# Row sums of a 64 MiB array: one load in place of four for the first row, and a store split into 104 and 24 partitions

## The chip, the cores and the metric

The kernel runs on one core of one Trainium2 chip. The metric is the device time of one execution in microseconds (us); less is better. A core has five engines with instruction queues of their own: TensorE, VectorE (DVE in the profile), ScalarE (ACT), GpSimd (POOL) and SyncE (SP). Data moves between HBM and the on-chip memory (128 partitions) by 16 DMA engines. A DMA is issued by an instruction of an engine's queue; here SyncE issues all loads and the last store, ScalarE the other store.

## The reference

The input is 32 x 512 x 1024 numbers in float32 (67.11 MB), and each run of 1024 is summed:

```python
def reference(x: np.ndarray) -> np.ndarray:
    return np.sum(x, axis=-1).astype(np.float32)
```

There are 16,384 sums of 1024 numbers, 128 for each of the 128 partitions. Nearly all of the work is to read the input once.

## The kernel before, in words

The 16,384 rows are cut into two blocks (`BLOCKS`): the first with 112 rows for each partition, the second with 16. Within a block, partition p holds consecutive rows, so one partition's share of a load is one run of memory. `out_b` and `res` are a block's output in HBM and its tile of sums.

The first block is streamed in seven tiles of `G` = 16 rows for each partition (64 KB for each partition, 8 MiB together), through three buffers of the tile `xt`. The loads are issued by SyncE in the order of the code. The first three tiles find their buffers free; each later load waits until VectorE has summed the tile that was in its buffer (`rows_dve`, one `tensor_reduce` at line 43 for each tile). In the seventh tile ScalarE sums the last 7 rows (`rows_act`, line 51, one instruction with an accumulator for each row), and VectorE the first 9.

The first tile is loaded in two steps (lines 79 to 85). The first of its 16 rows comes by four loads: each takes every fourth partition, 32 in all, 4 KB from each. The fifth load brings the other 15 rows, 60 KB for each of the 128 partitions. All the other tiles of the first block come by a single load of 128 partitions.

After the seventh tile, ScalarE issues the store of the first block's sums (line 91): 128 partitions with 112 sums, 448 bytes, each. It follows ScalarE's own seven rows in ScalarE's queue, waits for VectorE's nine, and has other rows of ScalarE behind it. At that time the loads of the second block are still under way, so the store runs beside them, inside the stream.

The second block's 16 rows come by five loads that get smaller (9, 4 and 2 rows, then the last row in two parts at `CUT` = 544), so that little work is left when the last byte lands. VectorE and ScalarE share them. The last row is summed by VectorE with `pairs_dve` (line 59), and SyncE issues the last store (line 116).

The instructions are scheduled by a planner as written, with one change by hand: after compiling, the first `EARLY` loads of SyncE are taken from the body of the program and put into the entry block, ahead of SyncE's part of the barrier at the start:

```python
loads = [i for i in code if i.engine == sp][:EARLY]
for load in loads:
    assert load.opcode == "DMACopy" and not load.sync_info.on_wait
    code.remove(load)
...
code[at:at] = loads
```

`EARLY` is 5 before: the four loads of the first row and the load of the other 15. SyncE issues the loads of the second and third tile after the barrier.

Of the kernel before, what the change touches and what calls it, by code (L numbers as in the profile page):

```python
# [1 line left out]

# [4 lines left out]

F32 = mybir.dt.float32
ADD = mybir.AluOpType.add
COPY = mybir.ActivationFunctionType.Copy  # L10
X = mybir.AxisListType.X

BLOCKS = (112, 16)
G = 16
ACT_ROWS = 7
CUT = 544
EARLY = 5


@with_exitstack  # L20
def row_sums(
    ctx: ExitStack,
    tc: tile.TileContext,
    x: bass.AP,
    out: bass.AP,
):
    nc = tc.nc
    P = nc.NUM_PARTITIONS

    x_flat = x.flatten_outer_dims()  # L30
    R, D = x_flat.shape
    C = R // P
    assert R % P == 0 and sum(BLOCKS) == C
    out_flat = out.rearrange("a (b c) -> (a b c)", c=1)

    xpool = ctx.enter_context(tc.tile_pool(name="x", bufs=3))
    rpool = ctx.enter_context(tc.tile_pool(name="res", bufs=1))
    part = rpool.tile([P, 1], F32, name="part")
    seen = rpool.tile([P, 1], F32, name="seen")
    pairs = [rpool.tile([P, D // 2], F32, name=f"pairs{i}") for i in range(3)]  # L40

    def rows_dve(xt, res, j, n, c):
        nc.vector.tensor_reduce(  # L43
            out=res[:, c : c + n],
            in_=xt[:, j * D : (j + n) * D].rearrange("p (j d) -> p j d", d=D),
            axis=X,
            op=ADD,
        )

    def sum_act(v, acc):  # L50
        nc.scalar.activation(out=v, in_=v, func=COPY, accum_out=acc)  # L51

    def rows_act(xt, res, j, n, c):
        for i in range(n):
            sum_act(xt[:, (j + i) * D : (j + i + 1) * D], res[:, c + i : c + i + 1])

    def pairs_dve(xt, a, b, first, acc, pairs):
        h = (a + b) // 2
        nc.vector.tensor_tensor_reduce(  # L59
            out=pairs[:, 0 : h - a], in0=xt[:, a:h], in1=xt[:, h:b], scale=1.0, scalar=first,  # L60
            op0=ADD, op1=ADD, accum_out=acc,
        )

    def block(r0, n):
        x_b = x_flat[r0 : r0 + P * n].rearrange("(p c) d -> p (c d)", p=P)
        out_b = out_flat[r0 : r0 + P * n].rearrange("(p c) -> p c", p=P)
        return x_b, out_b, rpool.tile([P, n], F32, name=f"res{r0}")

    full = C - G
    done = 0  # L70
    for b, n in enumerate(BLOCKS):
        x_b, out_b, res = block(done * P, n)
        final = b == len(BLOCKS) - 1
        whole = n - G if final else n
        c = 0
        while c < whole:
            m = min(G, whole - c)
            xt = xpool.tile([P, G * D], F32, tag="xt", name="xt")
            parts = [(slice(None), 0, m)]
            if done + c == 0:  # L80
                parts = [(slice(q, P, 4), 0, 1) for q in range(4)] + [(slice(None), 1, m)]
            for q, i, k in parts:
                nc.sync.dma_start(
                    out=xt[q, i * D : k * D], in_=x_b[q, (c + i) * D : (c + k) * D]
                )
            a = ACT_ROWS if done + c + m == full else 0
            rows_dve(xt, res, 0, m - a, c)
            rows_act(xt, res, m - a, a, c + m - a)
            c += m
        if not final:  # L90
            nc.scalar.dma_start(out=out_b, in_=res)
        done += n

    xt = xpool.tile([P, G * D], F32, tag="xt", name="xt")
    cuts = [0, 9, 13, 15]
    for i, k in zip(cuts, cuts[1:]):
        nc.sync.dma_start(out=xt[:, i * D : k * D], in_=x_b[:, (c + i) * D : (c + k) * D])  # L97
    last = 15 * D
    for i, k in ((0, CUT), (CUT, D)):
        nc.sync.dma_start(  # L100
            out=xt[:, last + i : last + k],
            in_=x_b[:, c * D + last + i : c * D + last + k],
        )

    for i, k in zip(cuts[:2], cuts[1:3]):
        h = (k - i) // 2
        rows_dve(xt, res, i, h, c + i)
        rows_act(xt, res, i + h, k - i - h, c + i + h)
    pairs_dve(xt, 13 * D, 14 * D, 0.0, res[:, c + 13 : c + 14], pairs[2])
    rows_act(xt, res, 14, 1, c + 14)  # L110
    pairs_dve(xt, last, last + CUT, 0.0, part, pairs[0])


    nc.vector.tensor_copy(out=seen, in_=part)  # L114
    pairs_dve(xt, last + CUT, last + D, part, res[:, c + 15 : c + 16], pairs[1])
    nc.sync.dma_start(out=out_b, in_=res)


def kernel(tc: tile.TileContext, x: bass.AP, out: bass.AP):
    row_sums(tc, x, out)  # L120
    tc.close()
    tc.compile()  # L122

    sp = mybir.EngineType.SP
    fn = tc.nc.m.functions[0]
    entry, body = None, None
    for blk in fn.blocks:
        ops = [i for i in blk.instructions if i.engine == sp]  # L130
        if entry is None:
            entry = blk
        elif any(i.opcode == "DMACopy" for i in ops):
            body = blk
            break
    code = list(body.instructions)
# [4 lines that stand above are left out]
    body.instructions = code  # L141
    code = list(entry.instructions)
    at = next(k for k, i in enumerate(code) if i.engine == sp and i.opcode == "Drain")
    code[at:at] = loads
    entry.instructions = code

# [1 line left out]
_INS = ['x']  # L148
_OUTS = [((32, 512), 'float32')]


# [23 lines left out]
```

## Time and profile before

| What | us |
|---|---|
| Median of three runs | 163.91 (163.80 to 163.95) |
| The profiled execution's own time | 163.95 |
| Its span (first to last instruction) | 162.2 |
| VectorE busy | 121.5, 16 instructions |
| ScalarE busy | 17.2, 31 instructions |
| One `tensor_reduce` of a whole tile (line 43) | 17.22 |
| First of them starts | 23.59 into the span |
| Store of the first block issued (line 91) | 149.44, lands 7.6 later |
| Last store issued (line 116) | 159.82, lands 1.4 later |

The profile is taken in one execution, whose time is a little longer than its span, by what lies before the first and after the last instruction. Busy times of engines leave out the instructions that issue DMAs and that wait. The DMA share is the mean busy share of the 16 DMA engines; a packet is one partition's run of bytes in a load or store, or the 4 bytes with which a DMA engine reports that its part of a DMA is done. 2208 packets moved 67.18 MB in all. The queue q1 is that of SyncE's DMAs and q10 that of ScalarE's.

### The profile page before, as it was taken

The page shows a single profiled execution, that of the slowest core. Times are in us where ns is not written, and L with a number is a line of the kernel's source. Part 1 is how long each engine was busy: PE and PEld are TensorE (multiplying, and loading weights), DVE is VectorE, ACT ScalarE, POOL GpSimd, SP SyncE. Part 2 cuts the span into 40 slices and gives each one's busy share as a digit, 9 for nine tenths or more (in the row PEclk, how much of TensorE's full clock was granted, in tenths as well). Part 3 has the DMA queues.
Part 4 walks back from the last instruction along what each step waited for, and adds up shares of the span by engine and source line. Part 5 has one row for each costly group of instructions (what it writes and reads, how often), then busy time and mean ns, then how long its engine had stood idle before and what let it go on. Part 6 is the DMA issues. An engine that isn't in the chain of part 4 may idle for free.

```text
span 162.2 us, 126 instructions
## 1 busy us (share of the span) xinstructions
DVE 121.5 (75%) x16; ACT 17.2 (11%) x31; POOL 0.2 (0%) x4
## 2 busy tenths in 40 slices
DVE  0000019999599986999589994999949999598883
ACT  0000000000000000000000000000000000596892
POOL 0000000000000000000000000000000000000000
DMA  7999799889989979969969959969979979998991
GB/s 220 394 485 455 318 456 517 388 388 517 420 356 517 469 307 517 501 275 517 501 275 517 517 259 517 517 275 501 517 307 469 517 323 453 437 418 366 427 393 45
DMA packets 2208, 67.18 MB, mean 414 GB/s; under 512 B 544, under 2 KB 672, under 8 KB 928
## 3 DMA queue, kind: packets, MB, share of 16 engines
q1 hardware_dynamic: 2064, 67.12, 96.5%
q10 hardware_dynamic: 144, 0.06, 0.1%
HBM read 67.11 MB, written 0.07 MB: 414 GB/s over the span
## 4 chain that ended last, share of the span: by engine, by line
DMA 73%; DVE 22%; SPq 0%; issue 0%; DVEq 0%
DMA xt<-in_x_dram 73%; DVE res L43 21%; DVE pairs L59 1%; SPq L97 0%; DVE seen L114 0%; DVE part L59 0%; DVEq L122 0%; DVE res L59 0%
## 5 line engine op out<-in xcount | busy, mean ns | idle before, releaser
L43 DVE TENSOR_REDUCE res<-xt 128x16 f32<-128x16384 f32 (+3 forms) x9 | 119.8, 13309 | 38.0 <-DMA xt<-in_x_dram 38.0
L51 ACT ACT_TABLE_LOAD x1 | 1.3, 1283 | 139.8 <-DMA xt<-in_x_dram 139.8
L51 ACT ACTIVATE xt<-xt 128x1024 f32<-128x1024 f32 x15 | 15.6, 1043 | 2.2 <-DMA xt<-in_x_dram 2.1
L51 ACT ACTIVATION_READ_ACCUMULATOR xt<-xt 128x1 f32 x15 | 2.8, 187 | 0.0
L59 DVE CUSTOM_DVE_ANT_0 pairs<-xt 128x512 f32<-128x512 f32 (+1 forms) x2 | 1.1, 568 | 0.2 <-DMA xt<-in_x_dram 0.2
L59 DVE CUSTOM_DVE_ANT_0 pairs<-xt,part 128x240 f32<-128x240 f32 x1 | 0.5, 469 | 0.0
L114 DVE COPY seen<-part 128x1 f32<-128x1 f32 x1 | 0.2, 153 | 0.0
L59 DVE DVE_READ_ACCUMULATOR2_ANT res<- 128x1 f32 x2 | 0.2, 84 | 0.0
L159 POOL MEMSET const-bfloat16-1.0<- 128x1 bf16 x1 | 0.1, 102 | 0.0
L159 POOL MEMSET const-uint8-127<- 128x1 uint8 x1 | 0.1, 102 | 0.0
L159 POOL MEMSET const-float32-0.0<- 128x1 f32 x1 | 0.1, 99 | 0.2 <-issue 0.2
L159 POOL MEMSET const-float32-1.0<- 128x1 f32 x1 | 0.1, 99 | 0.0
L59 DVE DVE_READ_ACCUMULATOR2_ANT part<- 128x1 f32 x1 | 0.1, 84 | 0.0
## 6 DMA issues: line engine op xcount, KB each, us to landing
xt<-in_x_dram SPq DMA_DIRECT2D x1, 7680.0 KB, 21.0
xt<-in_x_dram SPq DMA_DIRECT2D x1, 4608.0 KB, 32.4
xt<-in_x_dram SPq DMA_DIRECT2D x1, 2048.0 KB, 36.9
xt<-in_x_dram SPq DMA_DIRECT2D x1, 1024.0 KB, 39.0
xt<-in_x_dram SPq DMA_DIRECT2D x4, 128.0 KB, 2.5
xt<-in_x_dram SPq DMA_DIRECT2D x1, 272.0 KB, 39.2
xt<-in_x_dram SPq DMA_DIRECT2D x1, 240.0 KB, 39.3
xt<-in_x_dram SPq DMA_DIRECT2D x6, 40.8
```

The costliest lines, as they stand in the source:

```text
L43: nc.vector.tensor_reduce(out=res[:, c : c + n], in_=xt[:, j * D : (j + n) * D].rearrange("p (j d) -> p j d", d=D), axis=X, op=ADD,)
L51: nc.scalar.activation(out=v, in_=v, func=COPY, accum_out=acc)
L59: nc.vector.tensor_tensor_reduce(out=pairs[:, 0 : h - a], in0=xt[:, a:h], in1=xt[:, h:b], scale=1.0, scalar=first, op0=ADD, op1=ADD, accum ...
L114: nc.vector.tensor_copy(out=seen, in_=part)
L159: nc = _bacc.Bacc("TRN2", target_bir_lowering=False, num_devices=1)
```

## The change

Two places change. The first row of the first tile is loaded by one load of all 128 partitions, 4 KB each, in place of four loads of every fourth partition; the load of the other 15 rows is as it was, and `EARLY` goes from 5 to 2, so that the entry block again holds the loads of the first tile. The store of the first block is split in two, both issued by ScalarE one after the other: partitions 0 to 103, and partitions 104 to 127.

```diff
-EARLY = 5
+EARLY = 2
...
-            parts = [(slice(None), 0, m)]
-            if done + c == 0:
-                parts = [(slice(q, P, 4), 0, 1) for q in range(4)] + [(slice(None), 1, m)]
-            for q, i, k in parts:
+            parts = (0, 1, m) if done + c == 0 else (0, m)
+            for i, k in zip(parts, parts[1:]):
                 nc.sync.dma_start(
-                    out=xt[q, i * D : k * D], in_=x_b[q, (c + i) * D : (c + k) * D]
+                    out=xt[:, i * D : k * D], in_=x_b[:, (c + i) * D : (c + k) * D]
                 )
...
         if not final:
-            nc.scalar.dma_start(out=out_b, in_=res)
+
+            for i, k in ((0, 104), (104, P)):
+                nc.scalar.dma_start(out=out_b[i:k], in_=res[i:k])
```

In the queues, SyncE has two loads ahead of the barrier in place of five, and the rest of its order is the same; ScalarE has one DMA issue more, straight behind the first. VectorE, TensorE and GpSimd have the same instructions as before in the same order.

## The prediction

> **What bounds the kernel now.** I read the page's chain that ended last first, then the stretches of time by DMA share, then SyncE's issues at the start, then the packet records of the trace (each DMA packet with start, duration and bytes; quoted in words).
>
> ```profile
> DMA 73%; DVE 22%; SPq 0%; issue 0%; DVEq 0%
> ...
> q1 hardware_dynamic: 2064, 67.12, 96.5%
> q10 hardware_dynamic: 144, 0.06, 0.1%
> ```
>
> The chain is a load 73% of the time. The 22% of VectorE in it are not a limit: they are the reductions that free a buffer for a load which then stands in the queue behind two others. The load queue q1 fills 96.5% of 16 engines' time; the store queue q10 next to nothing. By stretches (columns: from:to, length, busy us of VectorE, ScalarE, GpSimd, TensorE clock, DMA share, GB/s; a packet is counted where it starts, so a stretch can exceed 1):
>
> ```profile
> 0.00:1.30 1.30, 0.00 (x0) 0.00 (x0) 0.20 (x4) 1.00 0.00 0
> 1.30:3.70 2.40, 0.00 (x0) 0.00 (x0) 0.00 (x0) 1.00 0.71 207
> 3.70:8.40 4.70, 0.00 (x0) 0.00 (x0) 0.00 (x0) 1.00 1.09 424
> 23.40:42.80 19.40, 17.22 (x1) 0.00 (x0) 0.00 (x0) 1.00 1.00 432
> 42.80:62.10 19.30, 17.22 (x1) 0.00 (x0) 0.00 (x0) 1.00 1.00 435
> ```
>
> Once it streams, all 16 engines are busy all the time (share 1.00, 432 to 435 GB/s) and VectorE needs 17.22 us of a 19.35 us period. So 1 us lost by the engines at the start is never won back, and 1 us won there should reach the end. The start is where they are idle: nothing for 1.3 us, then 207 GB/s for 2.4 us. The reason is in SyncE's issues (start, length, both in us):
>
> ```profile
> 0.00 0.55 SPq L83 DMA_DIRECT2D xt<-in_x_dram  x1
> 0.60 0.58 SPq L83 DMA_DIRECT2D xt<-in_x_dram  x1
> 1.22 0.59 SPq L83 DMA_DIRECT2D xt<-in_x_dram  x1
> 1.86 0.59 SPq L83 DMA_DIRECT2D xt<-in_x_dram  x1
> 2.49 0.58 SPq L83 DMA_DIRECT2D xt<-in_x_dram  x1
> ```
>
> One issue each 0.62 us. The first four bring 128 KB each, two 4 KB packets per DMA engine; a 4 KB packet takes 0.159 us once an engine is running (packet records), so 0.32 us of work arrives each 0.62 us. The fifth, with the 15 rows that keep the engines busy (61,440 B a packet, 2.267 us at full speed), starts only at 2.49.
>
> **What the Trainium skill says.** "DMA: Bandwidth & Descriptors", section on why a DMA increments its semaphore by 16: a DMA from SyncE or ScalarE runs on the largest number of engines up to 16 that divides its partition count, the lowest-numbered ones, one completion write each. That makes 16 engines for 128 and 32 partitions, 13 for 104, 12 for 24. The trace agrees for 128: q10's 144 packets are 128 rows and 16 completions. No run yet shows 13 or 12. The same page, section on latency, has about 0.6 us to a first byte on this path; here the first packet starts 1.32 us after the first issue starts, 0.77 after it ends, and the trace's number is used. Its section on bandwidth gives 435 GB/s for the 16 ports, which the 432 to 435 above agree with.
>
> **The start, worked out.** Removed: three issues of SyncE at 0.62 us. The first issue becomes one load of 128 rows of 4 KB, eight packets per engine; the big load's issue moves from 2.49 to about 0.60. It passes no other queue's work, and the barrier and the two loads behind it come 1.9 us earlier too, where they only wait in the queue.
>
> 1. Before, the big load's first packets start 3.77 to 4.69 us into the span (1.28 to 2.20 after its issue) and are slow: 2.3 to 3.1 us in place of 2.267. Subtracting 2.267 from their ends gives the time from which each engine is in effect streaming: 4.33 to 5.02. The same spread is still there at 139 us (the last 64 KB packets end from 138.44 to 139.16), and it is the latest engine that completes every load. So 5.02 is the number to beat.
> 2. After, the big load's packets are available from 0.60 + 1.28 = 1.9 to 2.8 us. An engine first has eight 4 KB packets, 8 x 0.159 = 1.27 us, so the big load is ready before they are done, and the row no longer starves.
> 3. The latest engine's start is the uncertain term. Dear end: the one-row load starts as the big load did, its last engine in effect at 5.02 - 2.49 = 2.53 after its issue. Then the big packets stream from 2.53 + 1.27 = 3.80: a gain of 5.02 - 3.80 = 1.22 us. Cheaper: engines start from 1.32 to 1.32 + 0.93 (the big load's spread of first packets), plus about 0.15 for a slow first packet as in the small loads (0.19 to 0.36 in place of 0.159): 2.40 + 1.27 = 3.67, gain 1.35. Cheapest: spread 0.25 as a 32-row load, 1.57 + 0.15 + 1.27 = 2.99, gain 2.0.
>
> I take 1.3: a load over 128 partitions has shown the spread of 0.93.
>
> **The store, worked out.** The 112-column store from ScalarE becomes 104 + 24 partitions. Its packets are 448 B, 25 ns each in the records, and lengthen the period of the 8 KB rows they alternate with from 0.309 to 0.327: about 18 ns each. Before, each engine has 8 and a completion, about 0.15 us. After, 12 engines have 10 and two completions (+0.04), the thirteenth as before, the last three none (-0.15). If those three are the latest, as a load handed out engine by engine would make them, up to 0.15 is gained; if the latest is another, 0.04 is lost. I take -0.05. Below zero this part can't give more than its whole, 0.15.
>
> The added issue on ScalarE (0.37 us, the first one's duration) has cover:
>
> ```profile
> 149.44 0.37 ACTq L91 DMA_DIRECT2D out_dram<-res  x1
> 150.51 4.42 DVE L43 TENSOR_REDUCE res<-xt 128x4 f32<-128x4096 f32 x1 [1.16 <-DMA xt<-in_x_dram]
> 150.56 1.06 ACT L51 ACTIVATE xt<-xt 128x1024 f32<-128x1024 f32 x1 [2.09 <-DMA xt<-in_x_dram]
> ```
>
> The first issue ends at 149.81, the next row of ScalarE waits for its data until 150.56; a second issue with its gap ends near 150.3. Without that cover six rows would be up to 0.4 late, and the final store would still have about 0.2 left, since ScalarE's last row is done about 0.6 before VectorE's last sum.
>
> **The end.** From the last load's landing (159.26) the tail is fixed: last sum 0.47, final store issued at 159.82 and about 1.4 to land. It moves with the stream.
>
> **Sum.** -1.30 - 0.05 = -1.35 us against the profiled execution's 163.95 us (span 162.2 and 1.75 around it): 162.6. The median of the three is 163.91, 0.04 lower, within the rounding: **162.6 us**.
>
> **Rivals.**
> - The start gains as above, 1.1 to 1.6: 162.3 to 162.8. Chance 0.65. For it: the starved 2.4 us, and the spread kept to the end.
> - Gain of the start larger, engines starting nearly together (1.6 to 2.0): 161.9 to 162.3, chance 0.06.
> - Only part arrives, 0.35 to 1.1: the slow first big packets (up to 0.80 over 2.267) come again behind the small ones, as a cost of first touching the data and not of a late descriptor. 1.35 less 0.80 is 0.55: 163.4, and with less of it 162.8 to 163.4. Chance 0.13. Against it: later 64 KB packets from other rows have at most 2% over their median.
> - Nothing, within 0.33 us of 163.91: the row's eight packets take so long that the early big load does not matter. Chance 0.06.
> - Slower: small packets by all 16 engines at once. The slowest 4 KB packets took 0.40 to 0.44, in the second load, where two loads met. If eight in a row cost 0.42 each the row takes 3.4 us in place of 1.27: 2.1 lost against 1.35 gained, 164.7. It decides from a mean of (1.27 + 1.35) / 8 = 0.33 us per packet. Against it: the second packet of an engine in the same load took 0.156 to 0.159. Chance 0.10 with others on this side, of which the store run by very few engines is one: 104 rows on a single one would add about 96 x 18 ns = 1.7 us to that engine, 0.4 net.
>
> **How the numbers follow.** A measurement of this kernel can tell about 0.2% (0.33 us) from no change. Faster by more: 0.65 + 0.06 + 0.13 = 0.84; within: 0.06; slower: 0.10. The range takes in the larger gain down to 162.1 and the partial gain and part of the no-change case up to 163.7; about 0.17 is left outside.
>
> **What would show it.** Right: two SyncE issues at 0.00 and 0.60 with the two following loads near 1.6 and 2.0; DMA share near 1 from about 2.3 us on; first VectorE reduction at about 22.3 in place of 23.59; q1 with 2064 - 48 = 2016 packets and q10 with 128 + 13 + 12 = 153; the final store about 1.3 earlier than 159.82; steady periods still 19.35. Wrong: first reduction not earlier than 23.3 (the start), or an earlier first reduction with an end that is not (the stream or the store).

## The result and the profile after

Six runs of the changed kernel have a median of 162.23 us (162.15 to 162.37), six of the kernel before, run beside it, 163.99 us (163.80 to 164.40): a ratio of 0.9892, 95% interval 0.9879 to 0.9904. The profiled execution took 162.37 us against 163.95. Faster was forecast, 162.6 us; the gain against the profiled execution is 1.58 us in place of 1.35.

The chain and the queues on the page of the changed kernel:

```profile
DMA 75%; DVE 22%; SPq 0%; issue 0%; DVEq 0%
...
q1 hardware_dynamic: 2016, 67.12, 97.2%
q10 hardware_dynamic: 153, 0.06, 0.1%
```

A load still ends last, and the load queue is busy for 97.2% of a shorter span. The packet counts are those forecast: 48 fewer on q1 (three loads less, 16 completions each), and 153 = 128 + 13 + 12 on q10. In the trace 13 engines report to the first store's completion semaphore (the counter by which a DMA tells that it has landed) and 12 to the second's, as the Trainium skill has it ("DMA: Bandwidth & Descriptors", the section on why a DMA increments its semaphore by 16).

The same stretches of time as before (from:to, length, busy us of VectorE, ScalarE, GpSimd, TensorE clock, DMA share, GB/s):

```profile
0.00:1.30 1.30, 0.00 (x0) 0.00 (x0) 0.20 (x4) 1.00 0.38 47
1.30:3.70 2.40, 0.00 (x0) 0.00 (x0) 0.00 (x0) 1.00 1.47 602
3.70:8.40 4.70, 0.00 (x0) 0.00 (x0) 0.00 (x0) 1.00 0.96 418
22.30:41.70 19.40, 17.35 (x2) 0.00 (x0) 0.00 (x0) 1.00 1.00 432
41.70:61.00 19.30, 17.15 (x2) 0.00 (x0) 0.00 (x0) 1.00 1.01 435
```

The starved 2.4 us are gone (602 GB/s booked, since big packets that start there are counted whole, in place of 207), and packets already move in the first 1.3 us, where there were none. The steady stretches are what they were, 432 and 435 GB/s. SyncE's issues (start, length):

```profile
0.00 0.38 SPq L81 DMA_DIRECT2D xt<-in_x_dram  x1
0.43 0.42 SPq L81 DMA_DIRECT2D xt<-in_x_dram  x1
1.26 0.33 SPq L81 DMA_DIRECT2D xt<-in_x_dram  x1
1.64 0.73 SPq L81 DMA_DIRECT2D xt<-in_x_dram  x1
```

The big load is issued at 0.43, not at 2.49. Each issue is also shorter than forecast, 0.38 and 0.42 in place of 0.55 to 0.59. In the packet records the first packet starts at 0.99 us (1.32 before); on every engine the first big packet starts right behind small ones, and 14 of these 16 take their full-speed 2.267 us. (The records do not name the engine. Here and below a packet is put to an engine by following each packet's end to the next one's start, 3 or 4 ns before it; where several ends fall together, that is an inference.) Around the store, in order of time:

```profile
148.11 0.98 ACTq L91 DMA_DIRECT2D out_dram<-res  x2
149.19 4.42 DVE L43 TENSOR_REDUCE res<-xt 128x4 f32<-128x4096 f32 x1 [1.16 <-DMA xt<-in_x_dram]
149.20 1.06 ACT L51 ACTIVATE xt<-xt 128x1024 f32<-128x1024 f32 x1 [2.19 <-DMA xt<-in_x_dram]
```

ScalarE's two issues end at 149.09, its next data lets it go on at 149.20: the cover held, with 0.1 us to spare. The first reduction and the last store, before:

```profile
23.59 17.22 DVE L43 TENSOR_REDUCE res<-xt 128x16 f32<-128x16384 f32 x1 [23.59 <-DMA xt<-in_x_dram]
...
159.82 0.35 SPq L116 DMA_DIRECT2D out_dram<-res  x1
```

and after:

```profile
22.08 17.22 DVE L43 TENSOR_REDUCE res<-xt 128x16 f32<-128x16384 f32 x1 [22.08 <-DMA xt<-in_x_dram]
...
158.36 0.35 SPq L116 DMA_DIRECT2D out_dram<-res  x1
```

The first reduction starts 1.51 us earlier, the last store 1.46. From the start of the first reduction to the end of the execution there are 162.37 - 22.08 = 140.29 us, 140.36 before. So 1.51 of the 1.58 us lie ahead of the first reduction, and 0.07 behind it, where the store is.

### The profile page after: what moved, and what is told of

Read it like the earlier page. It is cut to its first block, busy times and chain, and to the rows that moved or that the text cites. A ratio compares the mean times of both kernels' runs of the same rounds, so it can differ in the third digit from the quotient of the medians.

```text
span 160.6 us, 120 instructions
## 1 busy us (share of the span) xinstructions
DVE 121.4 (76%) x16; ACT 17.2 (11%) x31; POOL 0.2 (0%) x4
## 3 DMA queue, kind: packets, MB, share of 16 engines
q1 hardware_dynamic: 2016, 67.12, 97.2%
## 4 chain that ended last, share of the span: by engine, by line
DMA 75%; DVE 22%; SPq 0%; issue 0%; DVEq 0%
DMA xt<-in_x_dram 75%; DVE res L43 21%; DVE pairs L59 1%; SPq L97 0%; DVE seen L114 0%; DVE part L59 0%; DVEq L122 0%; DVE res L59 0%
```

## The experiments

They ran in three groups of four, each group on a chip of its own beside the kernel before, whose medians there were 164.27 us in the first group, 164.07 in the second and 164.15 in the third. A ratio is to the kernel before of the same group. In all of them but four_blocks, four_columns, store_only and the repeats, the ratio's interval excludes 1.

**Start alone** (label start_only): the changed kernel with the store whole.

```diff
-            for i, k in ((0, 104), (104, P)):
-                nc.scalar.dma_start(out=out_b[i:k], in_=res[i:k])
+            nc.scalar.dma_start(out=out_b, in_=res)
```

> The first row by one load, the store whole as before. Theory 1 (the gain is the start: the latest DMA engine streams about 1.5 us earlier, and the split store is worth at most its 0.15 us): 1.4 to 1.6 us below the kernel before, ratio 0.990 to 0.9915, and the first tile lands at 21.9 to 22.2. Rival (the split store gives a third of the gain or more, because the latest engines are those it leaves out): 0.9 to 1.2 us, ratio 0.9925 to 0.9945, with the same landing of the first tile.

Measured: 162.32 us (162.21 to 162.67), ratio 0.9875 (0.9846 to 0.9904). The first reduction:

```profile
22.03 17.22 DVE L43 TENSOR_REDUCE res<-xt 128x16 f32<-128x16384 f32 x1 [22.03 <-DMA xt<-in_x_dram]
```

That is the time and the start of the full change: the load of the first row brings the gain, by itself. The difference to the kernel before is 1.95 us, more than the 1.4 to 1.6 expected; the kernel before took 164.27 us here, 0.28 more than beside the changed kernel, which is most of the excess.

**Store alone** (label store_only): the kernel before with the split store.

```diff
-            nc.scalar.dma_start(out=out_b, in_=res)
+            for i, k in ((0, 104), (104, P)):
+                nc.scalar.dma_start(out=out_b[i:k], in_=res[i:k])
```

> The four loads of the first row as before, the store split into 104 and 24 partitions. Theory 1: between 0.15 us faster and 0.05 us slower, ratio 0.999 to 1.0003, with the first tile landing at 23.4 as before. Rival (the store's split is worth 0.5 us): ratio 0.997.

Measured: 164.34 us (163.85 to 164.91), ratio 1.0002 (0.9981 to 1.0023). The rival's 0.997 lies outside. An effect of the forecast's 0.05 us is far below what this interval can tell: the split is worth nothing that can be measured here. The first reduction started at 24.06 us, not at the 23.4 expected, but it did so in an unchanged kernel too (24.05 in before_again, below).

**Four loads of neighbouring partitions** (labels four_blocks, and four_blocks_again for one more execution):

```diff
-                parts = [(slice(q, P, 4), 0, 1) for q in range(4)] + [(slice(None), 1, m)]
+                parts = [(slice(q, q + 32), 0, 1) for q in range(0, P, 32)] + [(slice(None), 1, m)]
```

> Four loads of the first row as before, but each of 32 neighbouring partitions in place of every fourth. Theory 1 (it is the number of issues ahead of the big load): within 0.3 us of the kernel before, big load issued at about 2.5 us. Rival (every fourth partition makes the issue slow, 0.55 to 0.59 us in place of 0.38 to 0.42): issues 0.42 us apart, big load issued at about 1.7 us, 0.6 to 0.9 us faster than before.

> Four loads of 32 neighbouring partitions once more, whose profiled execution took 163.46 us while its others had a median of 164.25. If the pace of the issues belongs to the kernel: issues 0.37 to 0.42 us and first packet at 0.99 us again. If it varies from execution to execution, possibly 0.55 to 0.59 us and 1.32 us this time, with a time of 164 us or more.

Measured: 164.25 us (163.04 to 164.76), ratio 0.9984 (0.9967 to 1.0002); the second time a single execution of 163.90. Both profiles have the quick issues (0.37 to 0.42 us), a first packet at 0.99 and 1.02 us and the big load issued at 1.80 and 1.82. So the quick issues came as the rival had it, the same both times, but its gain of 0.6 to 0.9 us did not: the big load was issued 0.69 us earlier than in the kernel before, and the median of 22 runs gained nothing clear. The two profiled executions are among the faster ones of this kernel (first reductions at 22.93 and 23.25 us), so they show a gain of the start that the median does not. The pace of the issues alone does not explain what the one-load start gains.

**Two loads, of every second partition and of neighbours** (labels two_loads and two_halves; `EARLY` = 3 in both):

```diff
-                parts = [(slice(q, P, 4), 0, 1) for q in range(4)] + [(slice(None), 1, m)]
+                parts = [(slice(q, P, 2), 0, 1) for q in range(2)] + [(slice(None), 1, m)]    # two_loads
+                parts = [(slice(q, q + 64), 0, 1) for q in (0, 64)] + [(slice(None), 1, m)]   # two_halves
```

> The first row by two loads of every second partition, the store whole. Theory 1 (what counts is how late the big load is issued): the big load issued at 0.9 to 1.25 us; each engine has 4 packets of 4 KB (0.64 us) for each issue of 0.45 to 0.62 us, so it hardly starves, and 1.0 to 1.5 us is gained, ratio 0.991 to 0.994. Rival (each load ahead costs its share, a third of the gain for each of the three): about 1.0 us at most gained, ratio 0.994 or more.

> The first row by two loads of 64 neighbouring partitions, the store whole. Seven engines of the run with two loads of every second partition waited idle for the big load until 4.4 to 5.1 us, although it was issued at 1.23. Theory A (the stepped partitions do it: slow issues, and what follows them is slow too): issues 0.42 us apart, big load issued at 0.85, no idle engine, 162.4 to 163.0 us. Theory B (it is the number of loads ahead of the big one, in whatever pattern): some engines idle between row 0 and the big load again, 164 us or more.

Measured: 165.08 us (ratio 1.0049, 1.0032 to 1.0066) and 164.76 us (1.0044, 1.0032 to 1.0056), both slower than the kernel before. The big load was issued at 1.23 us in both, half as late as in the kernel before, and yet seven engines got their first big packet only at 4.43 to 5.13 (two_loads) and 4.20 to 4.93 us (two_halves), when their small packets had been done since 3.47 and 3.75 at the latest. Both theories of two_loads fall, and so does theory A of two_halves, which blames stepped partitions; its theory B had the idle engines and the time right. The neighbours' issues took 0.55 to 0.59 us here, so stepping is not what makes an issue slow either.

**Cutting columns in place of partitions** (labels two_columns, `EARLY` = 3, and four_columns, `EARLY` = 5): every load covers all 128 partitions.

```diff
-            parts = (0, 1, m) if done + c == 0 else (0, m)
+            parts = [q * D // 2 for q in range(2 + 1)] + [m * D] if done + c == 0 else (0, m * D)
...
-                    out=xt[:, i * D : k * D], in_=x_b[:, (c + i) * D : (c + k) * D]
+                nc.sync.dma_start(out=xt[:, i:k], in_=x_b[:, c * D + i : c * D + k])
```

(four_columns has 4 in place of 2.)

> The first row by two loads again, but each of all 128 partitions and half of the row's columns (2 KB), so that every load gives each engine eight packets of its own partitions; the store whole. Theory C (what costs is to cut the 128 partitions over several loads, two loads of 64 cost 2.4 us against one): as with one load, 162.2 to 162.7 us, no engine idle between row 0 and the big load. Theory B (what costs is the number of loads ahead of the big one): engines idle until 4 us or later, 164 us or more.

> The first row by four loads of all 128 partitions and a quarter of the row's columns (1 KB) each; the store whole. As many issues as in the kernel before. Prediction's step (the pace of the issues ahead of the big load is what starves the engines): big load issued at 1.7 to 2.5 us, engines run dry, 163.5 to 164.3 us. Theory C (only a cut over partitions costs): 162.3 to 162.9 us.

Measured: 165.06 us (ratio 1.0057, 1.0039 to 1.0074) and 164.14 us (0.9988, 0.9966 to 1.0011). Two cuts of columns cost what two cuts of partitions cost, and four columns what four cuts of partitions cost: theory C falls, and the times go with the number of loads ahead of the big one, however they are cut. The four columns by themselves also fit the prediction's step (164.14 us lies in its 163.5 to 164.3). The two-column run does not, and is the clearest against the pace of issues as the whole reason. Its issues:

```profile
0.00 0.37 SPq L81 DMA_DIRECT2D xt<-in_x_dram  x1
0.42 0.42 SPq L81 DMA_DIRECT2D xt<-in_x_dram  x1
0.88 0.43 SPq L81 DMA_DIRECT2D xt<-in_x_dram  x1
```

and its stretches and first reduction:

```profile
1.30:3.70 2.40, 0.00 (x0) 0.00 (x0) 0.00 (x0) 1.00 1.37 510
3.70:8.40 4.70, 0.00 (x0) 0.00 (x0) 0.00 (x0) 1.00 0.88 301
```

```profile
24.81 17.22 DVE L43 TENSOR_REDUCE res<-xt 128x16 f32<-128x16384 f32 x1 [24.81 <-DMA xt<-in_x_dram]
```

The big load is issued at 0.88 us, only 0.45 later than in the changed kernel, and the first reduction is 2.73 us later. Four engines start the big load at 4.38 to 4.94, and its first packets there take 3.1 to 3.6 us. Eight others went from a small packet straight to the big load at 2.71 to 3.12, and their first big packets took 2.34 to 3.11 us all the same.

**No row ahead, and two rows ahead** (labels no_first_row, `EARLY` = 1, and two_rows; both with the store whole):

```diff
-            parts = (0, 1, m) if done + c == 0 else (0, m)
+            parts = (0, m)                                      # no_first_row
+            parts = (0, 2, m) if done + c == 0 else (0, m)      # two_rows
```

> All 16 rows of the first tile by one load, no small load ahead of it; the store whole. Theory 1 (only the time of the first packets counts): the load starts at 0.99 us and its packets arrive over 0.9 us; the latest engine streams in effect at about 2.2 us, against 3.46 - 1.27 = 2.2 with the row ahead: 162.2 to 162.6 us. Rival (the row ahead is the cover under which the descriptors of the big load arrive, and without it engines wait one by one): first packets 0.6 us or more over 2.42 and 163 us or more.

> The first two rows by one load of 128 partitions (8 KB each), then the other 14; the store whole. If one row in front (1.27 us of work for each engine) already covers the arrival of the big load, as the first big packets of 2.267 us say, nothing changes: 162.2 to 162.5 us. If the four engines that come to the big load 0.3 us late are late because the cover is short, 0.2 to 0.3 us faster: 162.0.

Measured: 162.45 us (162.30 to 162.63), and 162.20 us (162.14 to 162.27). Without a row ahead the first packets (64 KB) are slow, 2.5 to 3.4 us in place of 2.418, most of them as slow as the rival said, but the sum is theory 1's: the latest engine streams in effect from 2.02 us, and the time is about 0.2 us from the changed kernel's. A second row ahead changes nothing that this comparison can tell: 162.20 beside 162.32 and 162.23. No version beats the changed kernel clearly.

**The kernel before once more** (label before_again, one execution, no edit):

> The kernel before once more, for its start. If the slow issues (0.55 to 0.59 us) and the late first packet (1.32 us) belong to the kernel: the same again. If they vary from execution to execution: 0.37 to 0.42 us and a first packet at 0.99, as in the runs with one load, and a time up to 0.5 us lower.

Measured: 164.38 us, with the issues at 0.55 to 0.59 us and the first packet at 1.33 us again. The slow issues came again in this kernel; the 0.43 us over the first profile come later, with a latest engine that streams in effect from 5.42 us in place of 5.02.

**The store eight times** (label store_eight):

```diff
-            nc.scalar.dma_start(out=out_b, in_=res)
+            for _ in range(8):
+                nc.scalar.dma_start(out=out_b, in_=res)
```

> The first row by one load, and the whole 128-partition store issued eight times over (the same bytes each time), to price a store packet. By the prediction's 18 ns a packet, 7 x 8 packets and 7 completions more on every engine add 7 x (8 x 0.018 + 0.01) = 1.1 us: 163.4 us. If the store's packets are hidden, under 0.3 us more: 162.3 to 162.6. If ScalarE's eight issues (0.4 us each) hold up its rows of the second block: the seven more issues end at about 151.2 us, 2 us after the data is there, and the last store waits for ScalarE: up to 1.5 us more, with ScalarE's last row as the releaser of the last store.

Measured: 172.21 us. The price of a packet does not come out of it. SyncE's waits (waited for: us in total, times, longest):

```profile
SPq L81 <- DVE res L43: 68.9, 4, 17.3
SPq L100 <- DMA out_dram<-res: 39.1, 2, 36.4
```

The stores write the same bytes, so each waited until the one before had landed; and the two loads of the last row (line 100) waited for stores, which they have no data in common with: the wait of the first one, issued at 155.21, is on the completion semaphore that the first store uses. The experiment made a wait of its own and is inconclusive for the store's packets.

## Why the prediction was right, and where it was not

The table has every profile but store_eight's, from the packet records and the timeline, in us. "Last arrival" is the start of the big load's first packet on the engine that gets it last; "in effect" is the time from which the latest engine streams (end of its first big packet less 2.267 us; for no_first_row less 2.418, and it has one row more to move; for two_rows less 2.116, and it has one row less); "difference" is the execution less the first reduction.

| Kernel | loads ahead | big load issued | last arrival | in effect | first reduction | execution | difference |
|---|---|---|---|---|---|---|---|
| no_first_row | 0 | 0.00 | 1.83 | 2.02 | 21.71 | 162.30 | 140.59 |
| after | 1 | 0.43 | 3.50 | 3.50 | 22.08 | 162.37 | 140.29 |
| start_only | 1 | 0.42 | 3.46 | 3.46 | 22.03 | 162.37 | 140.34 |
| two_rows | 1 | 0.42 | 4.40 | 4.40 | 21.77 | 162.14 | 140.37 |
| two_columns | 2 | 0.88 | 4.94 | 6.22 | 24.81 | 165.05 | 140.24 |
| two_loads | 2 | 1.23 | 5.13 | 5.86 | 24.77 | 165.00 | 140.23 |
| two_halves | 2 | 1.23 | 4.93 | 5.47 | 24.08 | 164.65 | 140.57 |
| four_blocks | 4 | 1.80 | 3.69 | 4.33 | 22.93 | 163.46 | 140.53 |
| four_blocks_again | 4 | 1.82 | 4.06 | 4.65 | 23.25 | 163.90 | 140.65 |
| four_columns | 4 | 1.84 | 4.26 | 5.79 | 24.38 | 164.72 | 140.34 |
| before | 4 | 2.49 | 4.69 | 5.02 | 23.59 | 163.95 | 140.36 |
| before_again | 4 | 2.49 | 4.47 | 5.42 | 24.05 | 164.38 | 140.33 |
| store_only | 4 | 2.49 | 4.74 | 5.48 | 24.06 | 164.74 | 140.68 |

**That the start sets the end: right, and shown.** From the first reduction to the end the thirteen take 140.23 to 140.68 us while the executions differ by 2.91. And the latest engine sets the first reduction: where the big load has 15 rows, from "in effect" to the first reduction it is 18.57 to 18.63 us in ten profiles, two_loads alone has 18.91. (Its eight packets at 2.267 us are 18.14 of that.) What the latest engine loses at the start is not won back in any of these runs.

**The start's 1.30 us: the place right, the size 1.51, the terms met partly by luck.** The latest engine was forecast in effect at 5.02 - 1.30 = 3.72 and measured at 3.50. As step 2 had it, the big load was there before the small packets were done. Of step 3's terms, the first packet was forecast at 1.32 us and came at 0.99: 0.17 of this is the shorter issue (0.38 in place of 0.55), the rest the shorter time from its end to the packet (0.62 in place of 0.77). But it is not what moved the latest engine. In the changed kernel's profile that engine has its first small packet at 2.26 us, where the forecast's cheaper case had 1.32 + 0.93 = 2.25, and no slow packet behind it. In start_only every engine has its first packet by 1.37, and the latest engine's first two take 0.55 and 0.65 us, 0.88 more than at full speed where 0.15 was forecast. Both end at 3.5, and in store_eight, with the same start, the latest engine is in effect at 3.17. So the terms differ from profile to profile and were off in opposite ways; that their sum came within 0.3 us in the first two is partly luck.

**The price of loads ahead of the big one: wrong as a rule.** Step 2 put the big load's packets at 1.28 to 2.20 us after its issue, and the starved row down to the pace of issues. With no load ahead that nearly held (1.01 to 1.83 after the issue), and with one the small packets hid it. With two ahead the last packets arrive 3.7 to 4.1 us after the issue, and the time is above that of four. An earlier big load alone did not pay: four_blocks and four_columns issue it 0.7 us earlier than the kernel before, for nothing clear in the medians. That the change goes to a single load ahead, where the step does no harm, was the forecast's good fortune; for two loads the same step led to 1.0 to 1.5 us of gain expected, and 0.8 us was lost (165.08 against 164.27). Shown is that it is neither stepped partitions, nor a cut over partitions, nor the pace of issues alone. Why the big load's packets come late, on some engines only, behind two or more small loads stays open: what happens between an issue and its packets isn't visible in these traces. Three loads ahead were not tried.

**The slow first big packets: gone with one small load ahead, and cover is not the whole reason.** The rival that had them come again, for 0.55 us of gain in all, is refuted: behind a full row of small packets the big packets take 2.267 us. Of the big load's 128 packets (a few are missing from some records), those more than 2% slower than full speed are 1 in the changed kernel, 2 in start_only and none in two_rows; 15 to 17, about one for each engine, in the kernel before, store_only and four_blocks; 16 in no_first_row; 31 to 38 in two_loads, two_halves, two_columns and four_columns, where later packets are slow too. Small packets in front don't make the big ones fast by themselves: in two_columns and four_columns eight and ten engines went straight from a small packet to the big load, and took 2.34 to 3.38 us. What makes these packets slow stays open.

**The store's -0.05 us: not measurable.** Behind the first reduction the change gains 0.07 us, start_only 0.02; store_only reads +0.32 against before in single profiles, and 1.0002 in timed runs. The differences among unchanged stores spread over 0.4 us, so the price of 18 ns a packet was neither confirmed nor refuted. Of the forecast's two cases, the gain needs the latest engine to be one of the three without a store packet. In store_only's profile it very likely was not: the last of the first store's 13 completions comes 0.51 us behind the one before, the last of the second store's 12 comes 0.62 behind, and the last of the final load's 16 comes 0.70 behind, which is what one late engine that carries both stores would show.

**The issue's cover: right, tighter than forecast.** The first of the two stores took 0.63 us to issue in place of 0.37, the second 0.31; 0.1 us of cover was left, not 0.25.

**The slower rival** (small packets of 0.42 us in a row): the small packets took 0.22 us on average, below its point of 0.33. The first on an engine took up to 0.94, those behind it mostly 0.159. The forecast's reading of the kernel before, 0.40 to 0.44 us in the second load, was a little off: its slowest took 0.42, and there was one of that kind in the fourth load too.

## What to carry to other kernels

In a kernel that, like this one, streams with all DMA engines busy, look at when the latest engine begins to stream: here the start of the first tile's reduction told the end to within 0.45 us. To start such a stream, at most one small load over all partitions ahead of the big one, or the big one at once, was best here; do not cut the first row into several loads, and do not trust an earlier issue of the big load by itself without looking at when its packets arrive on every engine. A split of the store that should spare three engines some 0.15 us each, by the forecast's estimate, made no difference that could be measured.

## What the runs showed of the hardware that was not expected

The cost of small loads ahead of a big one is not monotonic: none gives 162.45 us, one 162.2 to 162.3, two 164.8 to 165.1, four 164.1 to 164.3. The issues of the first loads take 0.37 to 0.43 us in some kernels and 0.55 to 0.59 in others, the same again in the two kernels that were profiled twice, and the first packet follows at 0.98 to 1.02 or at 1.32 to 1.34 us; neither the step of the partitions nor the number of loads explains which. One-load starts also vary less: 162.15 to 162.67 over the 12 runs of after and start_only, 163.67 to 165.31 over 49 runs of the kernel before (163.80 to 164.40 over the six beside the changed kernel) and 163.04 to 164.76 over 22 of four_blocks.
